# A streaming softmax: loads in three parts, and stores that wait for most of the load queued ahead of them

## The chip, the cores and the metric

One core of one Trainium2 chip. The metric is device time in microseconds (us). Executions of the kernel before agree within 0.07%, so differences of a few us can be read. All runs were at a granted clock of 1.0. Ratios are the mean time of one kernel's runs over that of the other's of the same rounds, so they are not quite the ratio of the medians quoted.

## The reference

```
logits: (16, 256, 32768) float32, temperature 1.0
scaled = logits / temperature - max over the last axis
out    = exp(scaled) / sum(exp(scaled))
```

It is a softmax over 4096 rows of 32768 numbers: 537 MB are read and 537 MB written.

## The kernel before

Each row is split in two, so 8192 half rows make 64 tiles of 128 partitions x 16384 numbers (64 KB per partition, 8.4 MB). Three such buffers rotate. All transfers are issued by SyncE on one queue, in this order: store(t), load(t+2), store(t+1), load(t+3), and so on.

```python
_LOAD = 8192            # numbers per partition in one load: two loads of 32 KB a tile
_STORE = 16384          # one store of 64 KB per partition
_PIECES = (4096, 4096, 4096, 2048, 2048)     # pieces of compute
_ON_DVE = (4096, 4096, 2048, 0, 0)           # of each piece's scaling, VectorE's share
_END = 4096             # first and last tile: parts of 16 KB

def load(t):
    n = _END if t in (0, G - 1) else _LOAD
    for s in range(0, W, n):
        nc.sync.dma_start(out=buf[t % _BUFS][:, s : s + n], in_=x[...])
def store(t):
    n = _END if t == G - 1 else _STORE
    for s in range(0, W, n):
        nc.sync.dma_start(out=o[...], in_=buf[t % _BUFS][:, s : s + n])

def normalise(t):       # ... cut
    for k in range(K):
        nc.vector.tensor_reduce(out=nm[:, k : k + 1], in_=xc, axis=X, op=A.max, negate=True)
        nc.scalar.activation(out=xc, in_=xc, func=Exp, bias=nm[:, k : k + 1], accum_out=ssum[:, k : k + 1])
    # ... one-column statistics: the pieces' maxima and sums are combined into a factor f per piece
    for k in range(K):  # VectorE scales [a, b), ScalarE [b, c)
        nc.vector.tensor_scalar_mul(out=xs[:, a:b], in0=xs[:, a:b], scalar1=f[:, k : k + 1])
        nc.scalar.activation(out=xs[:, b:c], in_=xs[:, b:c], func=Copy, scale=f[:, k : k + 1])

for t in range(_BUFS):
    load(t)
for t in range(G):
    normalise(t)
    store(t)
    if t and t + _BUFS - 1 < G:
        load(t + _BUFS - 1)
```

## Time and profile before

| | before |
|---|---|
| time, median | 2496.03 us |
| VectorE, ScalarE busy | 63%, 55% |
| share of sixteen DMA engines' time filled by packets | 99.7% |
| rate over the span | 430 GB/s |

The kernel is bound by its DMA engines, whose packets fill 99.7% of their time; the prediction below shows the lines. Four stretches of the steady part serve for comparison later. Each line has the stretch, its length, the busy time and instructions of VectorE, ScalarE and GpSimd, TensorE's clock, the mean share of the DMA engines and the rate in GB/s:

```profile
500.00:1000.00 500.00, 321.18 (x247) 277.56 (x182) 0.00 (x0) 1.00 1.00 433
1000.00:1500.00 500.00, 318.49 (x246) 274.82 (x181) 0.00 (x0) 1.00 1.00 434
1500.00:2000.00 500.00, 317.19 (x239) 273.68 (x179) 0.00 (x0) 1.00 1.00 433
2000.00:2400.00 400.00, 253.76 (x200) 220.13 (x146) 0.00 (x0) 1.00 1.00 433
```

The rate is the same throughout. Two readings are used in all that follows. Both come from records in the same traces. The *landings* are sixteen times per transfer (3184 for the 199 transfers of before), which I read as one for each of the sixteen DMA engines; "lag" is the last of the sixteen minus the eighth. The *packet records* give the start, duration and size of every packet. The median packet of before takes 2418 ns for a 64 KB row, 1213 for a 32 KB row and 611 for a 16 KB row, and what a packet takes above that is called stretch. The packets of 4 bytes, as many as the landings, are called landing signals. A packet's record does not name its engine; an engine is followed from the end of one packet to the start of the next. The engine that lands last in nearly every transfer is called the slow engine, most of the others the fast ones.

### The profile page before, as it was taken

What the parts mean: (1) busy time and instruction counts of PE and PEld (TensorE: products, weight loads), DVE (VectorE), ACT (ScalarE), POOL (GpSimd) and SP (SyncE); (2) the same over time, 40 slices, a digit from 0 to 9 for tenths busy, and PEclk for the clock granted to TensorE, in tenths of its full rate; (3) what the DMA queues carried; (4) which work ended last, traced back from release to release, by engine and by line L of the source; (5) the groups of instructions that cost most, each with busy time, mean ns of one, the idle gap of its engine ahead of it and who ended that gap; (6) DMA issues with size and microseconds to landing.
All of it is one profiled execution on the core that took longest, in us unless ns stands there. A gap on an engine that the chain in (4) does not pass through costs nothing.

```text
span 2494.7 us, 2743 instructions
## 1 busy us (share of the span) xinstructions
DVE 1581.4 (63%) x1216; ACT 1367.8 (55%) x895; POOL 0.2 (0%) x4
## 2 busy tenths in 40 slices
DVE  7666566665765657656666566665766656666574
ACT  6555464554645546455464554645646556465463
POOL 0000000000000000000000000000000000000000
DMA  9999999999999999999999999999999999999998
GB/s 420 428 427 438 426 435 435 430 438 430 431 435 433 437 434 426 439 429 435 439 425 438 428 436 436 428 439 431 433 433 433 438 432 430 433 433 434 437 426 350
DMA packets 28678, 1073.93 MB, mean 430 GB/s; under 512 B 3184, under 2 KB 3184, under 8 KB 3184
## 3 DMA queue, kind: packets, MB, share of 16 engines
q1 hardware_dynamic: 28656, 1073.75, 99.7%
q14 instruction: 22, 0.18, 0.0%
HBM read 536.87 MB, written 536.87 MB: 430 GB/s over the span
## 4 chain that ended last, share of the span: by engine, by line
DMA 73%; ACT 13%; DVE 12%; another core or an unknown queue 1%; SPq 1%; issue 0%; ACTq 0%
DMA x<-in_logits_dram 64%; DVE nm L103 11%; DMA out_dram<-x 8%; ACT x L110 7%; ACT x L143 6%; SPq L71 0%; DVE f L135 0%; ACT ee L120 0%; DVE rS L134 0%; DVE Sh L82 0%; DVE ttj L123 0%; DVE Sh L79 0%; SPq L63 0%; ACTq L185 0%
## 5 line engine op out<-in xcount | busy, mean ns | idle before, releaser
L103 DVE TENSOR_REDUCE nm<-x 128x1 f32<-128x4096 f32 x318 | 1123.3, 3581 | 673.3 <-DMA x<-in_logits_dram 673.3
L110 ACT ACTIVATE x<-x,nm 128x4096 f32<-128x4096 f32 x318 | 965.4, 3036 | 1020.9 <-DVE nm L103 1020.9
L143 ACT ACTIVATE x<-x,f 128x2048 f32<-128x2048 f32 (+1 forms) x194 | 370.9, 1975 | 73.7 <-DVE f L135 73.7
L139 DVE TENSOR_SCALAR x<-x,f 128x4096 f32<-128x4096 f32 (+2 forms) x194 | 372.2, 1975 | 2.3
L123 DVE CUSTOM_DVE_ANT_0 ttj<-ee,ssum 128x5 f32<-128x5 f32 (+1 forms) x64 | 10.6, 166 | 196.7 <-ACT ee L120 196.7
L110 ACT ACTIVATION_READ_ACCUMULATOR x<-x,nm 128x1 f32 x318 | 59.3, 186 | 0.0
L120 ACT ACTIVATE ee<-nm,nMh 128x5 f32<-128x5 f32 (+1 forms) x64 | 18.1, 284 | 0.0
L135 DVE TENSOR_SCALAR f<-ee,rS 128x5 f32<-128x5 f32 (+1 forms) x64 | 14.8, 231 | 2.2
L134 DVE RECIPROCAL rS<-Sh 128x1 f32<-128x1 f32 x64 | 10.5, 164 | 2.2
L82 DVE TENSOR_TENSOR nMh<-nMh 128x1 f32<-128x1 f32 x64 | 10.2, 159 | 2.2
L82 DVE TENSOR_TENSOR Sh<-Sh 128x1 f32<-128x1 f32 x64 | 10.2, 159 | 2.2
L118 DVE TENSOR_REDUCE nMh<-nm 128x1 f32<-128x5 f32 (+1 forms) x64 | 10.1, 158 | 2.2
L79 DVE STREAM_SHUFFLE nMh<-nMh 128x1 f32<-128x1 f32 x64 | 9.7, 151 | 0.0
L79 DVE STREAM_SHUFFLE Sh<-Sh 128x1 f32<-128x1 f32 x64 | 9.7, 151 | 0.0
L110 ACT ACT_TABLE_LOAD x1 | 1.3, 1283 | 8.1 <-DMA x<-in_logits_dram 8.1
L123 DVE DVE_READ_ACCUMULATOR2_ANT Sh<- 128x1 f32 x64 | 5.3, 82 | 0.0
L79 DVE LOAD_MASK_SELECT Sh<-Sh x64 | 0.9, 14 | 2.8
L79 DVE LOAD_MASK_SELECT nMh<-nMh x64 | 0.9, 14 | 2.8
L171 POOL MEMSET const-bfloat16-1.0<- 128x1 bf16 x1 | 0.1, 102 | 0.0
L171 POOL MEMSET const-uint8-127<- 128x1 uint8 x1 | 0.1, 102 | 0.0
L171 POOL MEMSET const-float32-1.0<- 128x1 f32 x1 | 0.1, 99 | 0.0
L171 POOL MEMSET const-float32-0.0<- 128x1 f32 x1 | 0.1, 98 | 0.2 <-issue 0.2
## 6 DMA issues: line engine op xcount, KB each, us to landing
x<-in_logits_dram SPq DMA_DIRECT2D x124, 4096.0 KB, 48.9
x<-in_logits_dram SPq DMA_DIRECT2D x8, 2048.0 KB, 31.8
out_dram<-x SPq DMA_DIRECT2D x4, 2048.0 KB, 18.0
out_dram<-x SPq DMA_DIRECT2D x63, 38.6
```

The lines of the kernel that those rows point to most:

```text
L79: nc.vector.stream_shuffle(out=v[:, j + 1 : j + 2], in_=v[:, j : j + 1], mask=mask)
L82: nc.vector.tensor_tensor(out=v[:, j + 1 : j + 2], in0=v[:, j : j + 1], in1=v[:, j + 1 : j + 2], op=op,)
L103: nc.vector.tensor_reduce(out=nm[:, k : k + 1], in_=xc, axis=X, op=A.max, negate=True)
L110: nc.scalar.activation(out=xc, in_=xc, func=Exp, bias=nm[:, k : k + 1], scale=inv_t, accum_out=ssum[:, k : k + 1],)
L118: nc.vector.tensor_reduce(out=nMh[:, 0:1], in_=nm, axis=X, op=A.min)
L120: nc.scalar.activation(out=ee, in_=nm, func=Exp, bias=nMh[:, n_rounds : n_rounds + 1], scale=-1.0)
L123: nc.vector.tensor_tensor_reduce(out=ttj, in0=ee, in1=ssum, scale=1.0, scalar=0.0, op0=A.mult, op1=A.add, accum_out=Sh[:, 0:1],)
L134: nc.vector.reciprocal(out=rS, in_=Sh[:, n_rounds : n_rounds + 1])
L135: nc.vector.tensor_scalar_mul(out=f, in0=ee, scalar1=rS)
L139: nc.vector.tensor_scalar_mul(out=xs[:, a:b], in0=xs[:, a:b], scalar1=f[:, k : k + 1])
L143: nc.scalar.activation(out=xs[:, b:c], in_=xs[:, b:c], func=Copy, scale=f[:, k : k + 1])
L171: nc = _bacc.Bacc("TRN2", target_bir_lowering=False, num_devices=1)
```

## The change

The intent, as far as the code tells it: hold each store back until most of the load ahead of it is in, so that transfers follow each other in an orderly way, and cut the loads so that there is a point, three quarters in, on which to wait. The compute pieces were evened out as well.

```diff
-_LOAD = 8192
+_LOADS = (8192, 4096, 4096)
-_PIECES = (4096, 4096, 4096, 2048, 2048)
-_ON_DVE = (4096, 4096, 2048, 0, 0)
+_PIECES = (4096, 4096, 4096, 4096)
+_ON_DVE = (2560, 2560, 2560, 2560)
     def load(t: int) -> None:
-        n = _END if t in (0, G - 1) else _LOAD
-        for s in range(0, W, n):
-            nc.sync.dma_start( ... )
+        s = 0
+        for n in [_END] * (W // _END) if t in (0, G - 1) else _LOADS:
+            arrivals.append(nc.sync.dma_start( ... ))
+            s += n
     def store(t: int) -> None:
-            nc.sync.dma_start( ... )
+            ins = nc.sync.dma_start( ... )
+            if arrivals:
+                tc.add_manual_dep(
+                    ins.ins, arrivals[-2].ins.name, sync, reason="stores begin in turn"
+                )
+                arrivals.clear()
```

`arrivals[-2]` is, in all but the first and last tiles, the second of the three parts of the load queued just ahead of the store. When it has landed, 16 KB per partition of that load are still to come.

More of the change, by code (lines that the diff above doesn't have):

```diff
@@ L40 @@
     W = V // _SPLIT
-    assert sum(_PIECES) == W and len(_PIECES) == len(_ON_DVE)
+    assert sum(_LOADS) == sum(_PIECES) == W and len(_PIECES) == len(_ON_DVE)
     x = xf.rearrange("n (h v) -> (n h) v", h=_SPLIT)
@@ L60, in load @@
     def load(t: int) -> None:
-        n = _END if t in (0, G - 1) else _LOAD
-        for s in range(0, W, n):
-            nc.sync.dma_start(
-                out=buf[t % _BUFS][:, s : s + n],
-                in_=x[t * P : (t + 1) * P, s : s + n],
+        s = 0
+        for n in [_END] * (W // _END) if t in (0, G - 1) else _LOADS:
+            arrivals.append(
+                nc.sync.dma_start(
+                    out=buf[t % _BUFS][:, s : s + n],
+                    in_=x[t * P : (t + 1) * P, s : s + n],
+                )
             )
+            s += n
     def store(t: int) -> None:
@@ L70, in store @@
         for s in range(0, W, n):
-            nc.sync.dma_start(
+            ins = nc.sync.dma_start(
                 out=o[t * P : (t + 1) * P, s : s + n],
@@ L74, in store @@
             )
+            if arrivals:
+                tc.add_manual_dep(
+                    ins.ins, arrivals[-2].ins.name, sync, reason="stores begin in turn"
+                )
+                arrivals.clear()
+    arrivals = []
+    sync = mybir.DependencyInfo(
+        mybir.DependencyClass.Sync, mybir.DependencyReason.SCHED_ONLY
+    )
     def combine(v, op) -> None:
```

## The prediction

> **What bounds the kernel now.** I read the page's busy shares and its DMA lines first.
>
> ```profile
> span 2494.7 us, 2743 instructions
> DVE 1581.4 (63%) x1216; ACT 1367.8 (55%) x895; POOL 0.2 (0%) x4
> DMA packets 28678, 1073.93 MB, mean 430 GB/s; under 512 B 3184, under 2 KB 3184, under 8 KB 3184
> q1 hardware_dynamic: 28656, 1073.75, 99.7%
> ```
>
> VectorE and ScalarE idle for a third or more of the span. All data goes through one queue, whose packets fill 99.7% of sixteen DMA engines' time. Every logit is read and every result written once, so the bytes can't shrink. The question is whether the queue ever runs dry; the timeline of one tile answers it.
>
> ```profile
> 841.93 0.34 SPq L71 DMA_DIRECT2D out_dram<-x  x1
> 842.87 0.80 SPq L63 DMA_DIRECT2D x<-in_logits_dram  x2
> 852.54 8.75 DVE L103 TENSOR_REDUCE nm<-x 128x1 f32<-128x4096 f32 x2 [10.68 <-DMA x<-in_logits_dram]
> 862.23 8.80 DVE L103 TENSOR_REDUCE nm<-x 128x1 f32<-128x4096 f32 x3 [0.94 <-DMA x<-in_logits_dram]
> 875.79 5.79 ACT L143 ACTIVATE x<-x,f 128x2048 f32<-128x2048 f32 x3 [1.15 <-DVE f L135]
> 881.61 0.34 SPq L71 DMA_DIRECT2D out_dram<-x  x1
> ```
>
> Columns: start, duration, engine, line. The parts whose reduces start at 852.54 and 862.23 belong to a load issued a tile earlier, at 803.61. So the queue holds, in order: store(t), load(t+2), store(t+1), load(t+3). At 841.93, when a store is issued, a whole load (landing until 862.2) is still ahead of it: 20 us of reserve. The queue is never dry.
>
> The DMA landings, one record per DMA engine in the trace, give the steady sequence of the last engine: load parts landed at 891.23 and 900.91, a store at 881.54 and 920.25. So 9.69 us for a 32 KB part, 19.33 for a store, 38.70 per tile (16.78 MB, 434 GB/s). Over 64 tiles that is 2476.8 us. The rest of the span, about 18 us, is start, end and one slow DMA engine, which I found by comparing, in each transfer, the last of the 16 landings with their middle (eighth):
>
> ```
> a load's last part, last landing us   62.53   201.05   473.16   900.91   2027.10   2416.01
> last minus middle us                   0.34     2.96     3.54     5.49      9.39     11.35
> ```
>
> The lag grows in steps of 1.0 us, for instance at 842.86, 1076.04 and 1347.91, each within two microseconds of an 8 KB packet of the instruction queue (841.4, 1074.6, 1346.4). The slow engine's packets are otherwise no longer than the others': 1213 ns for a 32 KB row. It never idles, and from 240 us on it loses only these nine steps. **The kernel's end is the sum of that one engine's packets, plus its fetches.** Most of the other fifteen finish their loads 11 us ahead, and end up waiting for data to store.
>
> [...]
>
> **The change, part by part.**
>
> *Loads of 32, 16 and 16 KB per partition.* 62 of the 64 loads have their second half sent as two parts, so eight 32 KB rows per engine become sixteen of 16 KB. The last load of before is already in 16 KB parts: its landings run 2435.33 to 2454.82 after the part landed at 2435.33, four parts, 4.87 us each. Two such are 9.745 against 9.69 for one 32 KB part: 0.055 us per tile, times 62 = **+3.4 us**, on the path, since the slow engine has no idle time to hide it.
>
> *Compute pieces.* From the groups split by shape:
>
> ```profile
> L103 DVE TENSOR_REDUCE nm<-x 128x1 f32<-128x4096 f32 x194 | 851.4, 4416 | 673.3 <-DMA x<-in_logits_dram 673.3
> L110 ACT ACTIVATE x<-x,nm 128x4096 f32<-128x4096 f32 x194 | 719.3, 3708 | 1020.9 <-DVE nm L103 1020.9
> L139 DVE TENSOR_SCALAR x<-x,f 128x2560 f32<-128x2560 f32 x8 | 11.9, 1549 | 0.1
> L103 DVE TENSOR_REDUCE nm<-x 128x1 f32<-128x2048 f32 x124 | 277.0, 2276 | 0.0
> ```
>
> Two reduces of 2048 (4.55 us) become one of 4096 (4.42); five exponentials become four; scaling is 4 x 1.55 = 6.2 us of VectorE beside four pieces of 1536 on ScalarE, 5.95 us in the end tiles. After the 32 KB part lands at L+9.7 the four reduces run through to L+27.4, the last exponential and its read end at L+31.3, statistics take 1.4 and scaling 6: ready at about L+38.6, against 852.54 - 9.7 = 842.8 to 881.6, also L+38.8, now. Worth 0: the store isn't wanted before the next load ends. VectorE keeps eight large operations per tile, so its instruction fetches, which by their spacing of 6 to 7 tiles I hold to be the slow engine's steps, stay.
>
> *The wait.* In the built program the store of tile t+1 waits for the second part of load(t+2), and nothing else blocks: the added semaphore reuses are of transfers two tiles back. The store is ready 20 us before load(t+2) ends; it will now be issued when the slow engine has one 16 KB part, 4.87 us, still to move. Until store packets flow I count: packet end to landing 0.48 us (packet records against landings), landing to issue 0.1, issue to first packet 0.9 (in before a final store issued at 2466.04 finds fast engines idle, and their packets start between 2466.88 and 2467.03). Together 1.5 us. The slow engine thus keeps 4.87 - 1.5 = 3.4 us of reserve: **+0 us**. The load behind the store is issued within a microsecond after it; its buffer was freed a load earlier. The fast engines, once more than 3.4 us ahead, will stop and wait for the store; their lead stays near 3.4 instead of growing to 11. That costs nothing, because they don't set the end, and gains nothing, because the slow engine's packets don't get shorter when others pause.
>
> *Start and end.* First and last tiles keep their form. Store(0) is issued at about 57 instead of 38 us, still before load(2) ends at 62.5. The last store waits for three quarters of the last load. 0.
>
> Sum: 2496.0 + 3.4 = 2499.4. I add 0.6 for collisions, below: **2500**.
>
> **The rivals.**
>
> *The queue runs dry.* If the path from landing to store packets took longer than 4.87 us, each of 62 tiles would gain a gap: 1 us each is 2562. For it: the reserve falls from 20 us to 3.4. Against it: 1.5 us measured piece by piece, and even the first loads, from cold, took 1.0 us from issue (0.73) to first packet (1.75).
>
> *Re-alignment brings back collisions.* Early in before, with all engines close together, the last load packets stretch as stores begin: at 58.2 to 58.6 all sixteen took 0.4 to 1.0 us longer, and from 118 to 290 us some ten per tile by 0.1 to 1.2. The last engine's period was then 161.01 - 121.50 = 39.51 and 201.05 - 161.01 = 40.04, so 0.8 and 1.3 above 38.70; at a lag of 2.9 it was 38.75 and 38.84, and from 400 us 38.71. The new wait releases the fast engines together. If it holds the lag under 2, each tile pays about 1 us: 2560. Against it: the lag that it leaves, 3.4, is just above where the cost had gone, and the fast engines stand idle then, with no load packet to collide. A cost of 0.01 to 0.1 per tile (0.6 to 6 us) is what I expect; a full return is the main way to "slower".
>
> *Order gains.* Keeping engines in step, one might hope, speeds them up by separating reads from writes. For it: early stretches fall below 434 GB/s. Against it: with lags of 3 to 11 us the packets run at their shortest duration anyway. What could be won is the early excess, some 3 to 4 us: 2496. [...]
>
> **Range and chances.** The low end takes the packet cost as halved and a few microseconds of early collisions saved: 2494. The high end takes 0.15 us per tile of collisions (9 us) on top of 2499.4: 2509. Beyond 2546, "slower", needs 0.75 us per tile, which only the first two rivals give: 4%. "Faster" 1%. Same: 95%.
>
> **What would show it.** Landings of 4.87 us for each 16 KB part and a tile period near 38.76 on the last engine; lag levelling at 3 to 4 us instead of 11; SyncE's store waits now put down to the load; the queue's share of sixteen engines' span a little lower, from the fast engines' pauses only. I am wrong if the last engine shows a gap between a load's end and its store (first rival), if its 16 KB packets are stretched in every tile (second), or if its instruction-fetch steps change in number or move to an engine that has time to spare.

There is the 64 x 38.70 = 2476.8 us of the trace, which is above the 2446 us (2% off) that "faster" needs.

The trace of before has what the argument needs. The wait follows the slowest engine: of the part whose reduce starts at 852.54, the last landing is at 852.52, the eighth at 847.00. What is queued keeps flowing while SyncE waits: it issues nothing between 882.9 and 920.3, and parts land at 891.23 and 900.91. It also shows the slow engine while others pause, near the end: from 2464.4 to 2466.8 thirteen of the sixteen engines have no packet, and the one that the slow engine starts at 2464.03 takes 2418 ns, as elsewhere.

## The result, and the profile after

| | before | after |
|---|---|---|
| time, median | 2496.03 us | 2515.98 us (2515.36 to 2520.07) |
| ratio, 95% interval | | 1.0083 (1.0066 to 1.0101) |
| rate over the span | 430 GB/s | 427 GB/s |
| median time from a store's issue to its landing | 38.6 us | 24.4 us |

The kernel is 0.8% slower, 20 us, where I had predicted 4. It is under the 2% line, and outside my range of 2494 to 2509. The page of the changed kernel:

```profile
span 2514.7 us, 2804 instructions
DVE 1579.9 (63%) x1216; ACT 1368.6 (54%) x833; POOL 0.2 (0%) x4
q1 hardware_dynamic: 37584, 1073.76, 100.0%
```

The compute engines are as busy as before. The queue's packets fill 100.0% of the DMA engines' time, in a span 20 us longer, with the same bytes. So the engines did not pause more, as I had expected of the fast ones: packets took longer (from 400 to 2400 us a 64 KB packet takes 2461 ns in the mean and up to 3568, against 2419 and 2668 in before). The same four stretches of the changed kernel:

```profile
500.00:1000.00 500.00, 318.22 (x246) 275.04 (x168) 0.00 (x0) 1.00 1.00 428
1000.00:1500.00 500.00, 315.05 (x234) 269.86 (x163) 0.00 (x0) 1.00 1.00 428
1500.00:2000.00 500.00, 310.24 (x246) 268.20 (x166) 0.00 (x0) 1.00 1.00 427
2000.00:2400.00 400.00, 254.22 (x193) 220.04 (x135) 0.00 (x0) 1.00 1.00 428
```

428 against 433 is lost evenly all along. The waits of SyncE (who waited for whom, total us, times, longest), and then one tile of the timeline (start, duration, engine, line):

```profile
SPq L74 <- DMA x<-in_logits_dram: 2239.7, 62, 43.6
SPq L74 <- DVE x L152: 27.8, 5, 15.6
```

```profile
1018.20 0.34 SPq L74 DMA_DIRECT2D out_dram<-x  x1
1018.59 2.92 SPq L64 DMA_DIRECT2D x<-in_logits_dram  x3
1052.37 13.07 DVE L116 TENSOR_REDUCE nm<-x 128x1 f32<-128x4096 f32 x3 [10.72 <-DMA x<-in_logits_dram]
1057.31 0.34 SPq L74 DMA_DIRECT2D out_dram<-x  x1
```

The store now waits for the load, as built: the second part's last landing is at 1018.08, the issue at 1018.20. The last landing of the third part is at 1023.19, so the load has 5.0 us to go at the issue instead of 20. The period here is 1057.31 - 1018.20 = 39.11 us.

The packet records around that issue show the price. On the left the slow engine, followed packet by packet back from its last landing; on the right some of the fast ones, which finish their load 3 us before it:

```
slow engine (start us, size, ns)        fast engines
1018.890  16K   611                     1019.658  landing signal, then 1019.664  64K store, 2418
1019.497  16K   900   (+289)            1019.701  landing signal, then 1019.707  64K store, 2418
1020.393  16K   618                     1019.727  landing signal, then 1019.733  64K store, 2418
...                                     ... eleven of them between 1019.66 and 1019.97
1022.870  landing signal, then the store
                                        1036.562  64K store, their last, 2799   (+381)
                                        1036.606  64K store, their last, 2771   (+353)
                                        1036.642  64K store, their last, 2752   (+334)
```

As eleven fast engines turn from load to store within 0.3 us, the load packet then under way on the slow engine takes half as long again (900 ns instead of 611). Seventeen microseconds later, when the fast engines turn from store to load, their own last store packets are stretched (by 334 to 381 ns in the three lines above). There is no gap on the slow engine: here, and in every tile from 350 to 2400 us, its store starts 6 ns or less after its load's landing signal.

### The profile page after: what moved, and what is told of

It is laid out like the page before. It is cut to its first block, busy times and chain, and to the rows that moved or that the text cites. A ratio compares the mean times of both kernels' runs of the same rounds, so it can differ in the third digit from the quotient of the medians.

```text
span 2514.7 us, 2804 instructions
## 1 busy us (share of the span) xinstructions
DVE 1579.9 (63%) x1216; ACT 1368.6 (54%) x833; POOL 0.2 (0%) x4
## 4 chain that ended last, share of the span: by engine, by line
DMA 96%; SPq 2%; issue 0%; ACT 0%; DVE 0%; ACTq 0%
DMA x<-in_logits_dram 95%; SPq L64 1%; DMA out_dram<-x 1%; SPq L74 1%; ACT x L156 0%; DVE nm L116 0%; ACT x L123 0%; ACTq L198 0%; DVE f L148 0%; ACT ee L133 0%; DVE rS L147 0%; DVE Sh L95 0%; DVE Sh L92 0%; DVE ttj L136 0%; DVE Sh L136 0%
## 5 line engine op out<-in xcount | busy, mean ns | idle before, releaser
L123 ACT ACTIVATE x<-x,nm 128x4096 f32<-128x4096 f32 x256 | 949.1, 3708 | 1040.3 <-DVE nm L116 1040.3
L156 ACT ACTIVATE x<-x,f 128x1536 f32<-128x1536 f32 x256 | 382.3, 1564 | 73.5 <-DVE f L148 73.5
L152 DVE TENSOR_SCALAR x<-x,f 128x2560 f32<-128x2560 f32 x256 | 380.2, 1548 | 2.6 <-DVE f L148 0.4
L136 DVE CUSTOM_DVE_ANT_0 ttj<-ee,ssum 128x4 f32<-128x4 f32 x64 | 10.4, 162 | 222.5 <-ACT ee L133 222.5
L123 ACT ACTIVATION_READ_ACCUMULATOR x<-x,nm 128x1 f32 x256 | 47.7, 186 | 0.0
L133 ACT ACTIVATE ee<-nm,nMh 128x4 f32<-128x4 f32 x64 | 18.0, 282 | 0.0
L148 DVE TENSOR_SCALAR f<-ee,rS 128x4 f32<-128x4 f32 x64 | 14.7, 229 | 2.2
L147 DVE RECIPROCAL rS<-Sh 128x1 f32<-128x1 f32 x64 | 10.5, 164 | 2.2
L131 DVE TENSOR_REDUCE nMh<-nm 128x1 f32<-128x4 f32 x64 | 10.0, 157 | 2.2
## 6 DMA issues: line engine op xcount, KB each, us to landing
out_dram<-x SPq DMA_DIRECT2D x63, 24.4
```

Of the source, the lines that this page charges most:

```text
L133: nc.scalar.activation(out=ee, in_=nm, func=Exp, bias=nMh[:, n_rounds : n_rounds + 1], scale=-1.0)
L136: nc.vector.tensor_tensor_reduce(out=ttj, in0=ee, in1=ssum, scale=1.0, scalar=0.0, op0=A.mult, op1=A.add, accum_out=Sh[:, 0:1],)
L147: nc.vector.reciprocal(out=rS, in_=Sh[:, n_rounds : n_rounds + 1])
L148: nc.vector.tensor_scalar_mul(out=f, in0=ee, scalar1=rS)
```

## The experiments

The theories: **A**, the wait holds the fast engines close to the slow one and in step, and their common turns stretch its packets (my second rival, at a size I had not expected). **B**, the smaller packets or the third load cost more than I sized. **C**, the store comes too late into the queue, in proportion to how little is queued ahead of it. Later A was sharpened to **D**: it is the fast engines' reaching the end of what is queued that brings the cost, whatever makes the store late; against **E**, it is the wait on the load's semaphore as such.

The results together. "Lag" is the mean in 500 to 750 us and in 2000 to 2250 us; "stretch" is what the 64 KB packets took above 2418 ns in the same two stretches, in us per engine (250 us hold about 6.4 tiles). It is a sign that the turns are disturbed, and not the cost: most of these packets belong to the fast engines, and the cost is reckoned on the slow one, below. In e9 the loads are 64 KB packets too, and are counted.

| kernel | median us | before, same rounds | lag | stretch of 64 KB packets |
|---|---|---|---|---|
| before | 2496.03 | | 4.1, 10.1 | 0.05, 0.07 |
| after | 2515.98 | 2496.03 | 2.8, 2.8 | 1.75, 1.86 |
| e1_no_wait | 2498.36 | 2496.20 | 4.0, 8.6 | 0.06, 0.08 |
| e2_pieces_only | 2496.52 | 2496.20 | 4.6, 10.7 | 0.03, 0.05 |
| e3_wait_first | 2503.67 | 2496.20 | 4.1, 7.9 | 0.07, 2.27 |
| e4_wait_quarter | 2499.59 | 2496.20 | 3.8, 10.5 | 0.06, 0.07 |
| e5_wait_late | 2514.84 | 2495.97 | 0.5, 0.5 | 2.06, 2.25 |
| e6_more_dve | 2505.61 | 2495.97 | 6.7, 16.9 | 0.12, 1.66 |
| e7_big_pieces | 2494.34 | 2495.97 | 4.6, 9.3 | 0.02, 0.06 |
| e8_late_compute | 2684.25 | 2496.40 | 0.4, 0.4 | 5.25, 5.26 |
| e9_whole_loads | 2498.65 | 2496.40 | 3.8, 7.8 | 0.48, 1.34 |
| e10_late_store | 2516.01 | 2496.48 | 3.6, 3.6 | 2.34, 2.55 |
| e11_big_pieces_again | 2493.99 | 2496.48 | 4.2, 8.9 | 0.03, 0.04 |

**e1_no_wait.** The changed kernel with only the wait undone.

```diff
-            if arrivals:
-                tc.add_manual_dep(ins.ins, arrivals[-2].ins.name, sync, ...)
-                arrivals.clear()
```

> The changed kernel without the wait: three load parts and the new pieces stay. Theory A (the wait holds the fast DMA engines close to the slow one and lines them up, and their simultaneous turns from load to store and back stretch packets of the slow engine): 2499 to 2500 us, that is before plus 3.4 us for the smaller packets; the lag of the last engine grows to 11 us again. Theory B (more and smaller packets, or three load issues instead of two, cost more than I sized): about 2516, as with the wait. Theory C (the store reaches the rings too late, 4.87 us ahead of need): 2499 to 2500, like A.

Measured: 2498.36 us, 2.2 over before (I had 3.4 for the packets). B falls: of the 20 us, 2515.98 - 2498.36 = 17.6 are the wait's. The lag grows again, to 9.6, and the 64 KB packets are stretched no more than in before.

**e2_pieces_only.** Before, with the new compute pieces.

```diff
-_PIECES = (4096, 4096, 4096, 2048, 2048)
-_ON_DVE = (4096, 4096, 2048, 0, 0)
+_PIECES = (4096, 4096, 4096, 4096)
+_ON_DVE = (2560, 2560, 2560, 2560)
```

> The kernel before with the new compute pieces alone. A, B (packets) and C: within 1 us of before, 2495 to 2497, because the store is ready some 20 us before it can start. If it is over 2500, the compute pieces matter, which none of the theories says.

Measured: 2496.52, ratio 1.0001 (0.9986 to 1.0016). No effect of the pieces is seen.

**e3_wait_first.** The changed kernel, waiting for the first part, with half a load still queued.

```diff
-                    ins.ins, arrivals[-2].ins.name, sync, reason="stores begin in turn"
+                    ins.ins, arrivals[-3].ins.name, sync, reason="stores begin in turn"
```

> The changed kernel, but a store waits for the first (32 KB) part of the load only: 9.7 us of load remain queued on the slow engine instead of 4.87. A: fast engines are held only when they are more than 9.7 - 1.5 = 8.2 us ahead, which the lag in before reached at about 1600 us; so 2499.4 plus at most 0.27 us for each of the last 23 tiles, 2499 to 2507, no stretched packets in the first half of the trace, lag levelling near 8. B: 2516. C (cost by lateness of the issue in every tile): between 2503 and 2512, and the stretch present from the first tiles on.

Measured: 2503.67. This run holds its own control. Its four stretches:

```profile
500.00:1000.00 500.00, 320.85 (x247) 277.74 (x169) 0.00 (x0) 1.00 1.00 433
1000.00:1500.00 500.00, 317.62 (x245) 274.44 (x167) 0.00 (x0) 1.00 1.00 432
1500.00:2000.00 500.00, 315.97 (x235) 270.77 (x164) 0.00 (x0) 1.00 1.01 431
2000.00:2400.00 400.00, 250.54 (x204) 219.49 (x137) 0.00 (x0) 1.00 1.00 426
```

The last column is at before's level until 1500 us and falls to 426 at the end. The lag reaches 7.3 in the stretch from 1500 to 1750, and there the stretched 64 KB packets begin: 4 packets by over 100 ns in 1250 to 1500, 33 in 1500 to 1750, 72 in 2000 to 2250. The last engine's period from store landing to store landing is 38.90 us between 350 and 1400 us, and 39.19 between 1600 and 2400. The same wait instruction with the same packets costs nothing for the first half and 0.29 us per tile after the lag has grown to what is queued. C, which wants the cost from the first tile on, falls.

**e4_wait_quarter.** Loads of 16, 16 and 32 KB, waiting for the first: 14.5 us remain queued.

```diff
-_LOADS = (8192, 4096, 4096)
+_LOADS = (4096, 4096, 8192)
-                    ins.ins, arrivals[-2].ins.name, sync, reason="stores begin in turn"
+                    ins.ins, arrivals[-3].ins.name, sync, reason="stores begin in turn"
```

> Loads of 16, 16 and 32 KB, and a store waits for the first of them: 14.5 us of load remain queued. Same packets, same wait instruction. A: the lag never reaches 14.5 - 1.5 = 13 us, so no engine is ever held: 2499 to 2500, lag growing to 11 us. B: 2516. C: 2500 to 2508.

Measured: 2499.59, as A has it. The wait is there for every store, and costs 1.2 us at most, which is the distance to e1_no_wait, whose load parts come in another order.

**e5_wait_late.** Loads of 32, 24 and 8 KB, waiting for the second: 2.43 us remain.

```diff
-_LOADS = (8192, 4096, 4096)
+_LOADS = (8192, 6144, 2048)
```

> Loads of 32, 24 and 8 KB, a store waits for the first two: only 2.43 us of load remain queued on the slow engine. A: the fast engines are held from a lead of 0.9 us on, the lag levels near 1 us, every tile has collisions on the slow engine: 2520 to 2560. C (lateness): 2530 to 2570, with a gap on the slow engine between its load and its store. If only the packets counted (B): 2514 to 2518.

Measured: 2514.84. I missed this one on the low side: with half the reserve it costs no more than the change. The lag is held at 0.5 us, as A said, and stretched 64 KB packets are there from the start (63 in the first 250 us). The number falls where B had put it, but B had fallen with e1. So the cost did not grow as the reserve shrank; a table after e10 gives a likely reason.

**e6_more_dve** tests what makes the slow engine slow: before, with twenty one-element VectorE copies more per tile. By the 0.15 to 0.16 us that VectorE's one-column operations take in before, that is an estimated 3 us of its time per tile, and the store of before is ready some 19 us before the load ahead of it ends (881.61 against 900.91).

```diff
+        for _ in range(20):
+            nc.vector.tensor_copy(out=ttj[:, 0:1], in_=nm[:, 0:1])
         nc.vector.tensor_reduce(out=nMh[:, 0:1], in_=nm, axis=X, op=A.min)
```

> The kernel before with 20 more one-element copies on VectorE in each tile [...]. If the slow DMA engine is slow because it carries VectorE's instruction fetches, 1.0 us each, their number about doubles, from ten to twenty: 2504 to 2508, and the lag at the end grows to about 20 us. If the lag has another cause: 2496, unchanged.

Measured: 2505.61. The line of the instruction queue (packets, MB, share), which read 22 packets in before:

```profile
q14 instruction: 32, 0.26, 0.0%
```

Ten fetches more, and 9.6 us more. The lag reached 16.9, not 20, for a reason that I had not foreseen: at that lead the fast engines come near the end of what before's own order leaves queued, and the 64 KB packets are stretched from 1750 us on, without any added wait. So a part of the 9.6 us is this cost, and by these ten fetches and 9.6 us I estimate one fetch at somewhat less than a microsecond of time here.

**e7_big_pieces** and **e11_big_pieces_again**: before, with fewer VectorE instructions.

```diff
-_PIECES = (4096, 4096, 4096, 2048, 2048)
-_ON_DVE = (4096, 4096, 2048, 0, 0)
+_PIECES = (8192, 8192)
+_ON_DVE = (5120, 5120)
```

> The kernel before with two compute pieces of 32 KB per partition instead of five: 15 instead of 19 recorded VectorE instructions per tile. If VectorE's fetches set the slow engine: two fetches fewer, 2493 to 2495, faster than before by 1 to 3 us and the fastest of all kernels here. If not: 2496. If the longer compute (some 25 us after a load's last part instead of 19) is no longer hidden: above 2500.

> The kernel before with two 32 KB compute pieces, once more with five rounds, for its interval: 2493.5 to 2495, 1.6 us under before, every one of its runs under every run of before.

Measured: 2494.34 and 2493.99. All nine runs lie between 2493.66 and 2494.94, under every run of before in those rounds (2495.46 to 2497.05); the intervals of the ratio (0.9978 to 1.0008 and 0.9979 to 1.0004) still include 1. The instruction queue of e7:

```profile
q14 instruction: 15, 0.12, 0.0%
```

It is the fastest version I have, by 2 us. With seven fetches fewer than before, its gain fits what e6 shows from the other side; that the fetches make it is not shown apart from the longer pieces.

**e8_late_compute** was to make the store late without a wait: before, with four ScalarE copies of the tile onto itself.

```diff
+        if 0 < t < G - 1:
+            for k in range(4):
+                xc = xs[:, k * _END : (k + 1) * _END]
+                nc.scalar.activation(out=xc, in_=xc, func=Copy, scale=1.0)
         nc.scalar.activation(out=ee, ...)
```

> The kernel before, with no wait on a load and its own two 32 KB load parts, but with four extra ScalarE copies of a tile onto itself (4 x 3.7 = 14.8 us) ahead of the statistics, so that the store is ready about 54 us after its load began to land instead of 39; the load ahead of it ends at 58. The fast engines then run out of queued work at a lead of some 3 us, as with the wait. Theory D (the cost comes from fast engines reaching the end of what is queued, whatever delays the store): 2508 to 2516, with stretched 64 KB packets in every tile from about 350 us on, the lag levelling near 3 us. Theory E (the cost is of the wait on the load's semaphore itself, or of the kernel with the wait alone): 2495 to 2498, lag growing to 11 us. If ScalarE's extra work becomes the bound: more than 2520, with gaps on the slow engine.

Measured: 2684.25. The test failed: VectorE waits 17.09 us in each tile for the statistics behind the copies (1066.3 us in all) and, in the order of the program, begins the next tile's reduces only when it has scaled this one (at 1001.80 us, with no wait for a load), so compute became the bound, at 41.9 us per tile against the 38.70 of before's packets. Its only use is that all engines then run out of work in every tile and the 64 KB packets are stretched most of all, by 5.25 us per 250 us.

**e9_whole_loads.** Before with 64 KB loads in one part, so that compute starts later and the store is ready later.

```diff
-_LOAD = 8192
+_LOAD = 16384
 # and the pieces and shares of the changed kernel
```

> The kernel before with loads of 64 KB per partition in one part and four compute pieces of 16 KB. Packets: a whole load takes 19.33 us as a store does, 0.05 us per tile less than two 32 KB parts, so 3 us less: 2493 if nothing else happened. Theory D: all reduces start after the whole load, the store is ready some 48 us after its load began, so fast engines run out at a lead of about 8 us, which the lag reaches at about 1500 us: up to 0.27 us per tile in the last 25 tiles, 2493 to 2500, no stretched 64 KB packets before about 1400 us. Without D: 2492 to 2494.

Measured: 2498.65 (2495.73 to 2502.73), within D's range and above what the packets alone would make. The profiled run, the fastest of the four, has the lag levelling at 7.8 and 33 stretched packets in 1500 to 1750, after 3 in 1250 to 1500. The stretched packets of the first 750 us, which I had not foreseen, look like the early collisions of before, now on 64 KB loads.

**e10_late_store.** The mended form of e8: before's loads, pieces and waits, but a store is issued only after VectorE's first reduce of the next tile. Nobody does more work.

```diff
+            first = nc.vector.tensor_reduce(out=nm[:, k : k + 1], ...)
+            if k == 0 and t:
+                store(t - 1, first)      # adds a dependency of the store on `first`
+                if t > 1 and t + _BUFS - 2 < G:
+                    load(t + _BUFS - 2)
 for t in range(G):
     normalise(t)
-    store(t)
-    if t and t + _BUFS - 1 < G:
-        load(t + _BUFS - 1)
+store(G - 1)
```

> The mended form of the late-compute test. The kernel before with its own loads, pieces and no wait on a load's semaphore; a store is issued only after VectorE's first reduce of the next tile, some 53 us after its load began to land, so that packets can flow about 3.8 us before the slow engine's load ahead of it ends. No engine does more work. Theory D (fast engines reach the end of what is queued): no stretch until the lag reaches 3.8 us, at about 500 us, then 0.35 us per tile: 2508 to 2514, lag levelling at 3 to 4 us, stretched 64 KB packets from then on. Theory E (the cost is of the wait on the load's semaphore, or of the 16 KB parts together with it): 2495 to 2498, lag growing to 11 us.

Measured: 2516.01, as slow as the changed kernel. Its waits of SyncE, and then one tile of its timeline:

```profile
SPq L71 <- DVE nm L112: 2305.6, 63, 38.3
```

```profile
1012.68 8.74 DVE L112 TENSOR_REDUCE nm<-x 128x1 f32<-128x4096 f32 x2 [9.70 <-DMA x<-in_logits_dram]
1017.13 3.71 ACT L123 ACTIVATE x<-x,nm 128x4096 f32<-128x4096 f32 x1 [14.12 <-DVE nm L112]
1017.16 0.34 SPq L71 DMA_DIRECT2D out_dram<-x  x1
```

The store goes out at 1017.16, 0.03 us after ScalarE starts on the result of the first reduce. There are no 16 KB load parts in the steady tiles and no store waits for the semaphore of a load queued ahead of it (it depends on that load through VectorE alone, whose first reduce reads the load's first half). The reserve is about what the change leaves, the lag levels at 3.6, and the stretch is somewhat larger. E falls, and D stands, with e3, e4 and e6 beside it: what counts is how near the fast engines are to the end of what is queued ahead of the store when it is issued.

**One number orders the runs.** The landings also give, for each store, its *margin*: the time from its issue to the eighth engine's last landing of the load queued ahead of it. By the margin, between 350 and 2400 us (e8, bound by compute, and e9, with its 64 KB loads, left out):

| margin, us | tiles, all other runs | stretch per engine and tile, us | the slow engine's loss per tile, median us |
|---|---|---|---|
| 3 or more | 385 | 0.01 | 0.01 (29 tiles of e3) |
| 2.5 to 3 | 7 | 0.05 | |
| 2 to 2.5 | 70 | 0.16 | 0.50 (32 tiles of the changed kernel and e10) |
| 1.5 to 2 | 86 | 0.39 | 0.44 (55) |
| under 1.5 | 30 | 0.76 | 0.01 (15) |

"Loss" is what a tile, from one store's last landing to the next, takes above the usual tile of the same load parts without the effect (38.76 in e1, 38.70 in before). Before never goes under a margin of 7.9 and e1 never under 11.0; e3 falls under 3 from about 1550 us on, e6 from about 1820. The changed kernel, e5 and e10 all level at a mean of 1.7 to 1.9 us, though 5.0, 2.4 and 5.5 us of load are left on the slow engine; that fits e5's costing no more. And the loss is not the stretch: where the margin is least, the stretch is largest and the slow engine loses nothing.

## Why the prediction was wrong

**The bound and the slow engine: right.** The end is set by one DMA engine's packets plus its fetches: more VectorE instructions made it later, with a larger lag (e6), and fewer made it some 2 us earlier, with a smaller one (e7, e11; the intervals include 1). Nine times in before, beside an 8 KB packet of the instruction queue that itself took 0.31 us, the slow engine fell back by 0.9 to 1.0 us. One reading is wrong without harm: the landing at 2435.33, called a part's, is a store's.

**The packets, +3.4 us: right in kind, a little high for this kernel.** e1 measured +2.2, e4, with the same sizes in another order, +3.4.

**The compute pieces, 0: right.** e2 measured +0.3, inside the spread.

**The wait, "+0 us": this is the step that failed.** Its measured parts held: landing to issue was 0.12 us (counted 0.1), a load's or store's last packet ended 0.46 us before its landing in the median of before (0.35 to 0.59 for nine in ten; counted 0.48), the lag levelled at 2.8 where I had said "near 3.4", and the slow engine shows no gap between its load and its store, so the first rival did not come. What failed is the sentence that holding the fast engines "costs nothing, because they don't set the end". It made the slow engine's packets longer. By landings between 350 and 2400 us, mean interval on the last engine, with the same packets:

```
us per transfer      after     e1_no_wait    difference
32 KB part           9.715     9.705         0.01
first 16 KB part     4.895     4.869         0.03
second 16 KB part    5.078     4.864         0.21
store               19.534    19.455         0.08
sum                                          0.33
```

The same reckoning for e10 against before gives 0.36, of which 0.28 lies in the second 32 KB part (9.971 against 9.687).

From 350 us to the end of the last load at 2475 there are about 54 tiles of 39.2 us, and 54 x 0.33 = 18 us, against 17.6 measured. Most of it sits in the part of the load that the slow engine still moves while the fast ones start the store, the place shown in the packet records above.

**The rival that came.** I had "re-alignment brings back collisions" and gave it 0.01 to 0.1 us per tile, with two arguments. One was that the lag left by the wait lies "just above where the cost had gone". That read the lag as the cause, and e3 refutes it: its stretched packets come at a lag of 7 to 8, and e6's at 16. The other was that the fast engines would stand idle "with no load packet to collide"; it forgot that the slow engine's last load packets were there to be hit. With the size that was measured, the rival gives 2499.4 + 18 = 2517, so the mechanism was on the list and its size was wrong by a factor of three to thirty. Nothing in the profile of before could have told 0.33 from 0.05, because in its steady part before never brings its fast engines near the end of the queue (its margin is never under 7.9 us). That was the reason to make the range wider: before's quiet came from a condition that the change removes.

**What stays open.** Why a turn costs more once the fast engines come near the end of what is queued, and why the slow engine loses nothing in the tiles with the least margin. Being close together is not enough. At the first two stores of before, e1, e4 and e7, ten of the sixteen engines began their last store packets within 0.2 to 0.3 us of each other, and the stretch was 0.00 to 0.03 us per engine and tile; in 31 tiles of the changed kernel that landed as closely it was 0.31. The load packets of such early tiles were stretched in some kernels (0.28 us per engine and tile in before from 60 to 120 us, the early collisions of the prediction) and hardly in e4 (0.05). Nor do the records show much of a pause. At 352.8, the first time that the fast engines catch up with the queue, four of them wait up to 0.1 us for their first store packet, and 17 us later fifteen engines' last store packets take 0.2 to 1.1 us more; in the tile at 1018 no fast engine pauses at all, and the cost is there.

## What to carry to other kernels

When the DMA engines are the bound, as here (99.7% of their time), look at each engine's landings, not at the queue's share: in before the engines drifted apart, and the last of the sixteen landings came 0.34 us after the eighth at 62.5 us and 11.35 us after it at 2416. What the slowest engine had still to move when a store was issued had to exceed the fast engines' lead by some 3 us here (an estimate from the margins of the table above), and not just the delay between a wait and the first packet (1.5 us in the prediction). The wait of the changed kernel issued each store "in time" for the slowest engine, which shows no gap over 6 ns, and still too late for the others, and that cost the slowest one as well (0.33 us per 8.4 MB load and store). The same wait one part earlier was free until the lead had grown (e3, to about 1500 us), and with 14.5 us left it cost 1.2 us at most (e4), so if an order of transfers is needed, wait on the earliest part that gives it, as far as these two runs tell.
